# Two group norms of a hybrid encoder layer, by ones products over high and low parts of the squares

## The chip, the core and the metric

The kernel runs on one NeuronCore of one Trainium2 chip. The metric is the device time of one execution in microseconds (us); shown is the median of several runs. The engines are TensorE (PE: products, with its weight loads as PEld), VectorE (DVE), ScalarE (ACT), GpSimd (POOL), and SyncE (SP), which issues most of the DMAs.

## The reference

One layer of an encoder over 512 tokens of width 2048. A normed input is multiplied by one wide matrix, and its columns split into an attention group (8 heads of 128) and a recurrent group (LRU, width 1024), each with a gate. What matters here is the end of the layer, where each group's output is normed over its own 1024 features before the gate and the output projection:

```python
def rms_norm(x, w):
    xf = x.astype(jnp.float32)
    y = xf * lax.rsqrt(jnp.mean(xf * xf, axis=-1, keepdims=True) + EPS)
    return (y * w.astype(jnp.float32)).astype(x.dtype)
...
    mixed = jnp.concatenate([rms_norm(attn_out, attn_norm_w) * jax.nn.silu(g_attn),
                             rms_norm(lru_out, lru_norm_w) * jax.nn.silu(g_lru)], axis=-1)
    return x + jnp.einsum('bse,ed->bsd', mixed, w_out)
```

So for each group and each token, the squares of 1024 features are summed, and the features are scaled by one over the root of their mean plus EPS.

## The kernel before

Both groups are held with features on the 128 partitions and the 512 tokens along the free dimension: `hp` (four pairs of tiles, LRU) and `ap_` (four pairs, attention). A product of f32 precision is made of three products of rounded parts: a tile is split into a high part (a cast to fp32r, by ScalarE) and a low part (the rest, a subtraction by VectorE), and `mm3` (lines 153 to 155) multiplies high by high, high by low and low by high. Weights are loaded by SyncE (`wraw`, line 206) in chunks of two blocks and split the same way in `wsplit` (lines 218 and 219) into `wh` and `wl`, four buffers each in a pool; the splits are issued with raised priority.

TensorE's order is written out by hand: the generators of the big projections (`proj_feat`, `proj_tok`) yield after every six products, and `weave` runs a chain of smaller work between these steps; a chain that yields n lets n steps of the projection go by. The order of ScalarE, VectorE and GpSimd in the stages of this change is that of a planner, which goes by priority and expected times; `tc.high_priority()` raises the priority, and `tc.issue_after` (`behind` for several) puts an instruction behind another of its engine. In the last stage (`outputs`), all engines follow the written order.

The sums of squares come first. For the LRU group, `lru_squares` (lines 560 to 570) adds the squares of `hp` and leaves `sums["l"]`, 128x512; its last addition is on GpSimd (line 570). For the attention group, each head's `values` adds its squares to `sums["a"]` on GpSimd (line 753). What is left is the sum over the 128 partitions, for every token.

`group_rstd` (line 816) does this by four f32 products, one for every 128 tokens: 128 columns of the sums are the loaded weights, and a column of ones moves (line 820). The result has tokens on partitions, four columns. It is copied out of PSUM (line 824), and `rsqrt_mean` (lines 346 and 347) makes the root of the mean on GpSimd with a power of -0.5. Then `rows` (line 352) turns the four columns into a row that stands on all partitions: it splits them into a high and a low part (lines 357 and 358), spreads each over a diagonal of 128x512 (line 360, by the identity), multiplies both diagonals with ones (line 367) and copies the result into `gbc` (line 368). `normed` (line 831) multiplies a pair by `gbc`.

For the LRU group this runs in the chain `kv` (line 655) beside the projection of q: `group_rstd` stands behind the splits of the two key heads (`split_head`), four steps later `rows`. For the attention group it runs in `later` (line 1342) beside the projection of the last gate: two steps, `group_rstd`, four steps, `rows` and the scaling of two pairs, four steps, and the gate with its Silu (`gate`, line 807). `seven` (lines 844 to 852) splits and combines the normed groups for the output stage. The input's norm (`xstats`, line 371) uses `rsqrt_mean` and `rows` too.

GpSimd also issues DMAs that add blocks of `w_out` in DRAM (line 902), each behind the last of certain GpSimd instructions (`last_pool`, set in `rsqrt_mean` and at line 708).

Of the kernel before, what the change touches and what calls it, by code (L numbers as in the profile page):

```python
# [12 lines left out]
F32R = mybir.dt.float32r  # L13
AF = mybir.ActivationFunctionType
# [3 lines left out]
P = 128  # L18
SEQ = 512
DM = 2048  # L20
KT = DM // P
NT = SEQ // P
HD = 128
NH = 8
NKV = 2
G = NH // NKV
NB = 8
EPS = 1e-6
# [35 lines left out]
def hybrid_kernel(  # L64
# [20 lines left out]
    nc = tc.nc  # L85
# [4 lines left out]
    pools, order = {}, {"left": [], "right": []}  # L90

    def opened(name, side):
        pools[name] = tc.alloc_tile_pool(name=name, bufs=1, side=side, reuse_waits="tile")
        order[side].append(name)
        return pools[name]
# [22 lines left out]
    def nm(s):  # L118
        cnt[0] += 1
        return f"{s}_{cnt[0]}"  # L120
# [22 lines left out]
    def mm():  # L143
        return ps.tile([P, SEQ], F32, tag="mm", name=nm("mm"))

    def const(shape, name, dt=F32):
        return cp.tile(list(shape), dt, tag=name, name=name)

    def f(ap):
        return ap.bitcast(F32)  # L150
# [9 lines left out]
    ones = const([P, P], "ones")  # L160
    nc.gpsimd.memset(ones, 1.0)
    ones_r = const([P, P], "ones_r", F32R)
# [80 lines left out]
    def behind(those):  # L243
        stack = ExitStack()
        for ins in those:
            stack.enter_context(tc.issue_after(ins))
        return stack
# [52 lines left out]
    def in_order(v):  # L300
        return v.rearrange("p (t i r) -> p i t r", t=NT, i=NQ)
# [42 lines left out]
    def rsqrt_mean(dst, src, n, width):  # L344

        nc.gpsimd.tensor_scalar(dst, src, 1.0 / n, EPS, op0=ALU.mult, op1=ALU.add)
        last_pool[0] = nc.gpsimd.tensor_tensor(dst, dst, nhalf[:, :width], op=ALU.pow).ins
# [4 lines left out]
    def rows(dst, col, dg):  # L352

        shape = [P, NT, P]
        part = [const([P, NT], nm("part")) for _ in range(2)]
        parts = [dg() for _ in part]
        nc.vector.tensor_copy(part[0].bitcast(F32R), col)
        nc.vector.tensor_sub(part[1], col, part[0])
        for c, d in zip(part, parts):
            nc.vector.tensor_mul(  # L360
                d, ident[:, None, :].broadcast_to(shape), c[:, :, None].broadcast_to(shape)
            )
        yield
        pb = mm()
        for k, d in enumerate(parts):
            d = d.rearrange("p t q -> p (t q)")
            nc.tensor.matmul(pb, ones_r, d, start=k == 0, stop=k == 1)  # L367
        nc.vector.tensor_copy(dst, pb)
        yield
# [59 lines left out]
    def drain(fill):  # L429
        for _ in fill:  # L430
            pass
# [30 lines left out]
    sums = {}  # L462
# [97 lines left out]
    def lru_squares():  # L560

        hsum = pools["rot"].tile([P, 2, SEQ], F32, tag="hsum", name="hsum")
        nc.scalar.activation(hsum, hp[0], AF.Square)
        for pair in hp[1:]:
            yield 2
            sq = pools["rot"].tile([P, 2, SEQ], F32, tag="hsq", bufs=1, name=nm("hsq"))
            nc.scalar.activation(sq, pair, AF.Square)
            nc.vector.tensor_add(hsum, hsum, sq)
        sums["l"] = hsum[:, 0, :]
        nc.gpsimd.tensor_add(sums["l"], sums["l"], hsum[:, 1, :])  # L570
# [29 lines left out]
    def norm_rope(es, nh, tab):  # L600

        es = [e[:, : nh * HD].rearrange("p (h d) -> p h d", d=HD) for e in es]
        rs = []
        for e in es:
            r = pools["rot"].tile([P, nh], F32, tag=f"rr{nh}", bufs=NT, name=nm("rr"))
            for h in range(nh):
                sq = pools["rot"].tile([P, HD], F32, tag="sh", bufs=1, name=nm("sh"))
                nc.scalar.activation(sq, e[:, h, :], AF.Square, accum_out=r[:, h : h + 1])
            rsqrt_mean(r, r, HD, nh)
            rs.append(r)  # L610
        for t, (e, r) in enumerate(zip(es, rs)):
            sq = pools["rot"].tile([P, nh, HD], F32, tag="sq", bufs=2, name=nm("sq"))
            nc.vector.tensor_mul(e, e, r[:, :, None].broadcast_to([P, nh, HD]))
            for s in range(2):
                nc.vector.tensor_mul(
                    sq.rearrange("p h (a s d) -> p h a s d", s=2, d=32)[:, :, :, s, :],
                    e.rearrange("p h (a s d) -> p h a s d", s=2, d=32)[:, :, :, 1 - s, :],
                    tab[:, t, 1, :].rearrange("p (a s d) -> p a s d", s=2, d=32)[:, None, :, s, :]
                    .broadcast_to([P, nh, 2, 32]),
                )  # L620
            nc.vector.tensor_mul(e, e, tab[:, t, 0, :][:, None, :].broadcast_to([P, nh, HD]))
            nc.vector.tensor_add(e, e, sq)
        return es

    kth, ktl = [None] * NKV, [None] * NKV
# [5 lines left out]
    def sent(es, nh, *us):  # L631

        us = us or [
            pools["rot"].tile([P, NQ, 2, NT, B], F32, tag="uq", bufs=2, name=nm("uq"))
            for _ in range(nh // 2)
        ]
        for n, u in enumerate(us):
            for t, e in enumerate(es):
                blocks(u, t, e[:, 2 * n : 2 * n + 2].rearrange("p h d -> p (h d)"))
            yield  # L640
            asides.append(put_aside(u, "qd", 5))

    def landed(aside_):

        to = pools["qkv"].tile([P, NQ, 2, NT, B], F32, tag="lq", bufs=2, name=nm("lq"))
        bring_back(to, aside_)
        return to

    def split_head(pair, k, hi, lo):
        src = pair[:, :, k]  # L650
        hi, lo = (in_order(v) for v in (hi, lo))
        nc.scalar.copy(hi, src)
        nc.vector.tensor_sub(lo, src, f(hi))

    def kv(es):
        turned_k = sent(norm_rope(es, NKV, rk), NKV)
        yield 20
        opened("wx", "right")
        for t in range(NT):
            vv = es[t][:, NKV * HD :]  # L660
            vt = aside(
                lambda *a: pools["qkv"].tile(*a, tag="v", bufs=NT, name=nm("v")), 2 * NKV * HD // H
            )
            vh[t], vl[t] = vt[:, 0, :], vt[:, 1, :]
            nc.scalar.copy(vh[t], vv)
            nc.vector.tensor_sub(vl[t], vv, f(vh[t]))
        yield from lru_squares()
        yield 2
        drain(turned_k)
        yield 6  # L670
        pair = landed(asides.pop(0))
        for h in range(NKV):
            yield (12, 4)[h]
            kt = pools["qkv"].tile([P, 2, SEQ], F32R, tag="kt", bufs=NKV, name=nm("kt"))
            kth[h], ktl[h] = kt[:, 0, :], kt[:, 1, :]
            split_head(pair, h, kth[h], ktl[h])
        r = group_rstd(sums["l"], "r_l", NB * P)
        yield 4
        drain(rows(
            gbc, r,  # L680
            lambda: pools["rope"].tile([P, NT, P], F32R, tag="kv", bufs=NT, name=nm("kv")),
        ))

    qs = {}

# [127 lines left out]
    def fin_s(shape=(P, SEQ), dt=F32):  # L813
        return pools["fin"].tile(list(shape), dt, tag="s", bufs=2, name=nm("s"))

    def group_rstd(src, name, n):

        pr = mm()
        for t in range(NT):
            nc.tensor.matmul(  # L820
                pr[:, t : t + 1], src[:, t * P : (t + 1) * P], ones[:, 0:1], start=True, stop=True
            )
        r = const([P, NT], name)
        nc.vector.tensor_copy(r, pr[:, :NT])
        rsqrt_mean(r, r, n, NT)
        return r

    gbc = const([P, SEQ], "gbc")

    def normed(pair):  # L830
        nc.vector.tensor_mul(pair, pair, gbc[:, None, :].broadcast_to([P, 2, SEQ]))
# [22 lines left out]
    def aside(tile_of, n):  # L854

        t = tile_of([P, n * H + 16], F32R)
        return t[:, 8 : 8 + n * H].rearrange("p (n e) -> p n e", e=H)
# [475 lines left out]
    def build(i, pair, parts):  # L1333
        mixed[i][1] = parts
        seven(pair, *parts)
# [4 lines left out]


    def later():
        yield 2
        with tc.high_priority():
            r = group_rstd(sums["a"], "r_a", NH * HD)
        yield 4
        with tc.high_priority():
            drain(rows(gbc, r, lambda: fin_s((P, NT, P), F32R)))
        for pair in ap_[:2]:
            normed(pair)  # L1350
        yield 4
        todo = gate(late, ap_[:2], R_AN, fin_s)
        for _ in range(3):
            yield next(todo)
        build(4, ap_[0], [hring.tile([P, 7, H], F32R, name=nm(t)) for t in ("mh", "ml")])
        yield from todo
        for pair in ap_[2:]:
            normed(pair)
# [78 lines left out]
```

## Time and profile before

| what | value |
|---|---|
| time, median of 3 runs | 631.11 us (630.88 to 631.38) |
| the profiled execution: time | 631.51 us |
| its span, first to last instruction | 629.7 us |
| PE, DVE, ACT, POOL busy, share of the span | 99%, 78%, 55%, 17% |
| mean granted TensorE clock | 0.998 |

A line of the profile names the engine, the line of the kernel and the operation, then output and inputs by the program's names, shapes and how many; L820 is line 820. A timeline has the start in us from the beginning of the span, the duration, and in brackets the idle time before it with what ended it. A view of waits has who waited for whom, us in total, how many times, and the longest. Matmuls are pipelined, so their durations overlap: the distance from start to start is what one costs.

### The profile page before, as it was taken

What the parts mean: (1) busy time and instruction counts of PE and PEld (TensorE: products, weight loads), DVE (VectorE), ACT (ScalarE), POOL (GpSimd) and SP (SyncE); (2) the same over time, 40 slices, a digit from 0 to 9 for tenths busy, and PEclk for the clock granted to TensorE, in tenths of its full rate; (3) what the DMA queues carried; (4) which work ended last, traced back from release to release, by engine and by line L of the source; (5) the groups of instructions that cost most, each with busy time, mean ns of one, the idle gap of its engine ahead of it and who ended that gap; (6) DMA issues with size and microseconds to landing.
All of it is one profiled execution on the core that took longest, in us unless ns stands there. A gap on an engine that the chain in (4) does not pass through costs nothing.

```text
span 629.7 us, 8304 instructions
## 1 busy us (share of the span) xinstructions
PE 623.8 (99%) x2771; PEld 514.4 (82%) x2771; DVE 491.2 (78%) x796; ACT 348.5 (55%) x612; POOL 104.0 (17%) x137
## 2 busy tenths in 40 slices
PE   9999999999999999999999999999999999999997
PEld 6888888888888888888888888888888888888885
DVE  5967979986699874987887888549978866886875
ACT  3764899379936812555475447435445633443441
POOL 0000210112003631622122232100310001010010
PEclk9999999999999999999999999999999999999999
DMA  8877676859774599489668646924995777896262
GB/s 286 286 225 235 176 195 174 177 137 194 235 233 135 170 250 233 100 209 272 190 166 250 201 142 192 263 72 130 238 236 187 212 251 243 286 320 235 68 200 100
DMA packets 73594, 127.61 MB, mean 203 GB/s; under 512 B 6616, under 2 KB 29264, under 8 KB 73552
## 3 DMA queue, kind: packets, MB, share of 16 engines
q1 hardware_dynamic: 65664, 109.65, 55.7%
q0 software_dynamic: 7712, 17.31, 14.4%
q8 instruction: 21, 0.34, 0.2%
q10 hardware_dynamic: 176, 0.14, 0.1%
q14 instruction: 21, 0.17, 0.1%
HBM read 110.29 MB, written 37.75 MB: 235 GB/s over the span
## 4 chain that ended last, share of the span: by engine, by line
PE 97%; DMA 1%; DVE 0%; SPq 0%; ACT 0%; issue 0%; DVEq 0%
PE pj L154 21%; PE pj L153 20%; PE pj L155 20%; PE mm L1026 14%; PE pj L1026 10%; PE mm L155 4%; PE mm L153 3%; PE mm L154 3%; DMA wr<-in_w_in_dram 1%; PE mm L253 0%; PE mm L820 0%; PE mm L367 0%; SPq L240 0%; DVE wl L219 0%; DVE cb L1057 0%; SPq L206 0%
## 5 line engine op out<-in xcount | busy, mean ns | idle before, releaser
L153 PE MATMUL pj<-x,wh 128*128 128x512 f32 x376 | 146.9, 391 | 0.0
L154 PE MATMUL pj<-x,wh 128*128 128x512 f32 x376 | 146.6, 390 | 0.2 <-DVE x L261 0.2
L155 PE MATMUL pj<-x,wl 128*128 128x512 f32 x376 | 146.3, 389 | 0.0
L218 ACT CAST wh<-wr 128x512 fp32r<-128x512 f32 x143 | 85.6, 617 | 95.6 <-PE pj L154 36.7
L219 DVE TENSOR_TENSOR wl<-wr,wh 128x512 fp32r<-128x512 f32 x144 | 100.1, 722 | 20.0 <-ACT wh L218 18.7
L878 ACT CAST wh<-wr 128x1024 fp32r<-128x1024 f32 (+1 forms) x72 | 60.7, 860 | 75.0 <-PE mm L1026 35.4
L879 DVE TENSOR_TENSOR wl<-wr,wh 128x1024 fp32r<-128x1024 f32 (+1 forms) x72 | 68.7, 984 | 30.1 <-ACT wh L878 30.0
L154 PEld LDWEIGHTS pj<-x,wh 128*128 128x128 f32 x376 | 70.6, 188 | 15.2 <-DVE x L261 0.6
L155 PEld LDWEIGHTS pj<-x,wl 128*128 128x128 f32 x376 | 70.6, 188 | 14.8
L153 PEld LDWEIGHTS pj<-x,wh 128*128 128x128 f32 x376 | 70.6, 188 | 14.8
L153 PE MATMUL pj<-wh,x 128*128 128x512 f32 x192 | 74.8, 390 | 0.0
L155 PE MATMUL pj<-wh,x 128*128 128x512 f32 x192 | 74.7, 389 | 0.0
L154 PE MATMUL pj<-wl,x 128*128 128x512 f32 x192 | 74.7, 389 | 0.0
L902 POOL DMA_DIRECT2D t<-in_w_out_dram x40 | 33.7, 904 | 143.4 <-DMA t<-in_w_out_dram 99.9
L1026 PE MATMUL mm<-wh,ml 128*128 128x512 f32 x128 | 49.8, 389 | 0.0
L1026 PE MATMUL mm<-wh,mh 128*128 128x512 f32 x128 | 49.8, 389 | 0.0
L1026 PE MATMUL mm<-wl,mh 128*128 128x512 f32 x128 | 49.8, 389 | 0.0
L154 PEld LDWEIGHTS pj<-wl,x 128*128 128x128 f32 x192 | 36.0, 188 | 7.5
L153 PEld LDWEIGHTS pj<-wh,x 128*128 128x128 f32 x192 | 36.0, 188 | 7.5
L155 PEld LDWEIGHTS pj<-wh,x 128*128 128x128 f32 x192 | 36.0, 188 | 7.4
L708 POOL TENSOR_SCALAR p<-p,sm 128x512 f32<-128x512 f32 x32 | 24.2, 759 | 90.0 <-DVE sm L707 90.0
L1026 PE MATMUL pj<-wh,mh 128*128 128x512 f32 x96 | 37.4, 389 | 0.0
(209 smaller groups left out, 1035.6 us busy)
## 6 DMA issues: line engine op xcount, KB each, us to landing
wr<-in_w_in_dram SPq DMA_DIRECT2D x71, 512.0 KB, 5.0
wr<-in_w_out_dram SPq DMA_DIRECT2D x24, 512.0 KB, 5.3
t<-in_w_out_dram POOLq DMA_DIRECT2D x40, 256.0 KB, 7.3
wr<-t SPq DMA_DIRECT2D x40, 256.0 KB, 5.5
pd<-u SPq DMA_DIRECT2D x16, 512.0 KB, 3.0
pt<-pd SPq DMA_DIRECT2D x64, 128.0 KB, 3.9
t<-in_w_out_dram SPq DMA_DIRECT2D x24, 256.0 KB, 5.4
t<-t SPq DMA_DIRECT2D x16, 256.0 KB, 5.4
```

The source lines that it names most:

```text
L153: nc.tensor.matmul(acc, lh, rh, start=start, stop=False)
L154: nc.tensor.matmul(acc, lh, rl, start=False, stop=False)
L155: nc.tensor.matmul(acc, ll, rh, start=False, stop=stop)
L218: copy(hi, raw[:, k, :]).ins,
L219: nc.vector.tensor_sub(lo, raw[:, k, :], f(hi)).ins,
L708: last_pool[0] = nc.gpsimd.tensor_scalar(p, p, sm, 0.0, op0=ALU.mult, op1=ALU.add).ins
L878: nc.scalar.copy(hi[:, to], b)
L879: nc.vector.tensor_sub(lo[:, to], b, f(hi[:, to]))
L902: nc.gpsimd.dma_start(dst, src, accum_op=ALU.add)
L1026: nc.tensor.matmul(dst[s], lh[:, ts_], rh, start=i == 0 and j == 0, stop=i == 7 and j == 2)
```

## The change

`group_rstd` goes. Its place is taken by two functions. `halved` splits the 128x512 sums into a high part (a copy into fp32r on ScalarE) and a low part (a subtraction on VectorE). `spread` multiplies both with a 128x128 block of ones into one bank of PSUM, so that every partition receives the sum of all; ScalarE takes the root of the mean plus EPS out of PSUM into `gbc`, with EPS from a constant tile, and VectorE takes the reciprocal in place, in four pieces of 128 tokens. `rows` stays for the input's norm.

In the LRU group the parts are made where `group_rstd` stood, pinned behind the split of the second key head, and `spread` stands where `rows` stood, four steps later. In the attention group the parts are made at the start of `later`, `spread` stands where `group_rstd` stood, and where `rows` stood there is nothing left. The parts use the buffers that the diagonals of `rows` used. The constant `eps` is 48 floats wide.

```diff
     def split_head(pair, k, hi, lo):
         src = pair[:, :, k]
         hi, lo = (in_order(v) for v in (hi, lo))
-        nc.scalar.copy(hi, src)
-        nc.vector.tensor_sub(lo, src, f(hi))
+        return nc.scalar.copy(hi, src).ins, nc.vector.tensor_sub(lo, src, f(hi)).ins
...
-            split_head(pair, h, kth[h], ktl[h])
-        r = group_rstd(sums["l"], "r_l", NB * P)
+            those = split_head(pair, h, kth[h], ktl[h])
+        parts = halved(
+            sums["l"],
+            lambda: pools["rope"].tile([P, SEQ], F32R, tag="kv", bufs=NT, name=nm("kv")),
+            those,
+        )
         yield 4
-        drain(rows(
-            gbc, r,
-            lambda: pools["rope"].tile([P, NT, P], F32R, tag="kv", bufs=NT, name=nm("kv")),
-        ))
+        spread(gbc, parts, NB * P)
...
-    def group_rstd(src, name, n):
-
-        pr = mm()
+    eps = const([P, 48], "eps")
+    nc.gpsimd.memset(eps, EPS)
+
+    def halved(src, tile_of, those=()):
+
+        hi, lo = tile_of(), tile_of()
+        with behind(those):
+            nc.scalar.copy(hi, src)
+            nc.vector.tensor_sub(lo, src, f(hi))
+        return hi, lo
+
+    def spread(dst, parts, n):
+
+        pb = mm()
+        for k, part in enumerate(parts):
+            nc.tensor.matmul(pb, ones_r, part, start=k == 0, stop=k == 1)
+        nc.scalar.activation(dst, pb, AF.Sqrt, scale=1.0 / n, bias=eps[:, :1])
         for t in range(NT):
-            nc.tensor.matmul(
-                pr[:, t : t + 1], src[:, t * P : (t + 1) * P], ones[:, 0:1], start=True, stop=True
-            )
-        r = const([P, NT], name)
-        nc.vector.tensor_copy(r, pr[:, :NT])
-        rsqrt_mean(r, r, n, NT)
-        return r
+            ts_ = slice(t * P, (t + 1) * P)
+            nc.vector.reciprocal(dst[:, ts_], dst[:, ts_])
...
     def later():
+        with tc.high_priority():
+            parts = halved(sums["a"], lambda: fin_s(dt=F32R))
         yield 2
         with tc.high_priority():
-            r = group_rstd(sums["a"], "r_a", NH * HD)
+            spread(gbc, parts, NH * HD)
         yield 4
-        with tc.high_priority():
-            drain(rows(gbc, r, lambda: fin_s((P, NT, P), F32R)))
         for pair in ap_[:2]:
             normed(pair)
```

## The prediction

> **What bounds the kernel now.** I read the page first: the span, the busy line and the head of the chain that ended last.
>
> ```profile
> span 629.7 us, 8304 instructions
> ...
> PE 623.8 (99%) x2771; PEld 514.4 (82%) x2771; DVE 491.2 (78%) x796; ACT 348.5 (55%) x612; POOL 104.0 (17%) x137
> ...
> PE 97%; DMA 1%; DVE 0%; SPq 0%; ACT 0%; issue 0%; DVEq 0%
> ```
>
> TensorE is busy for 623.8 of 629.7 us, and 97% of the chain that sets the end is TensorE. Busy alone would not prove that it never waits, so next I read the view of waits, for PE and for its weight loads (PEld):
>
> ```profile
> PE mm L1144 <- POOL ones L161: 1.1, 1, 1.1
> ...
> PEld mm L155 <- DVE q L653: 0.3, 1, 0.3
> ```
>
> The first row is the warm-up at the very start. After the pipeline has filled, TensorE waits nowhere for more than 0.3 us. So here the time is what TensorE has to issue: an instruction taken out of its stream is worth its whole slot, and anything else counts only if it makes TensorE wait. Both groups' norms stand in such a stream. The timeline of PE around the LRU group's norm, then around the attention group's (start, duration, instruction):
>
> ```profile
> 231.72 0.40 PE L155 MATMUL pj<-wh,x 128*128 128x512 f32 x1
> 231.96 0.95 PE L820 MATMUL mm<-ones,hsum 128*128 128x1 f32 x8
> ...
> 233.08 0.39 PE L154 MATMUL pj<-wl,x 128*128 128x512 f32 x1
> ...
> 238.33 0.62 PE L367 MATMUL mm<-kv,ones_r 128*128 128x512 f32 x2
> 238.79 0.40 PE L153 MATMUL pj<-wh,x 128*128 128x512 f32 x1
> ```
>
> ```profile
> 430.10 0.40 PE L155 MATMUL pj<-x,wl 128*128 128x512 f32 x1
> 430.33 0.95 PE L820 MATMUL mm<-ones,asum 128*128 128x1 f32 x8
> ...
> 431.45 0.39 PE L154 MATMUL pj<-x,wh 128*128 128x512 f32 x1
> ...
> 436.71 0.62 PE L367 MATMUL mm<-s,ones_r 128*128 128x512 f32 x2
> ```
>
> Durations of neighbours overlap, so the price of an instruction is read from starts, and that of an ordinary 128x512 product from twelve in one row of the chain (start, us):
>
> ```profile
> 472.71 2.72 PE mm L1026 x12
> ```
>
> That is 0.227 us each. What the reader is to see: the four products of line 820 stand in the stream as eight TensorE instructions, and although each moves a single column (128x1) they hold it for most of a microsecond.
>
> **The change part by part.** *TensorE, LRU group.* From the last product before line 820 (231.72) to the second after it (233.08) are 1.36 us; two ordinary starts take 2 x 0.227 = 0.45. Line 820 costs 0.91 us, and it goes. The two products of ones with the halves take the place and the form of line 367: from 238.33 to 238.79 are 0.46 us for the two, an ordinary slot each, as now. Saved: 0.91.
>
> *TensorE, attention group.* 430.10 to 431.45 are 1.35 us, less 0.45: 0.90. The two products move up from 436.71 to this place, at an unchanged price. Saved: 0.90. Together 0.91 + 0.90 = **1.81 us**. This is the only term that lies on the path by itself.
>
> *Are the halves there when TensorE asks?* The sums end early:
>
> ```profile
> L570 POOL TENSOR_TENSOR hsum<-hsum x1: 1622/1622/1622, 206.1 to 206.1; 128x512 f32<-128x512 f32 x1
> ...
> 422.73 1.30 POOL L753 TENSOR_TENSOR asum<-asum,p 128x512 f32<-128x512 f32 x1 [15.41 <-ACT p L752]
> ```
>
> Splitting costs one ScalarE copy and one VectorE subtraction; the same pair on 128x512 runs in every head's split:
>
> ```profile
> L652 ACT CAST q<-lq 128x512 fp32r<-128x512 f32 x8 | 4.9, 621 | 6.2 <-PE mm L155 6.2
> ...
> L653 DVE TENSOR_TENSOR q<-lq,q 128x512 fp32r<-128x512 f32 x8 | 5.3, 676 | 0.0
> ...
> 226.86 1.25 DVE L653 TENSOR_TENSOR kt<-lq,kt 128x512 fp32r<-128x512 f32 x2
> ```
>
> LRU: the sum has been there since 207.7; the halves are pinned behind the last key split, which VectorE ends at 228.1, so they are due near 230, and TensorE asks at 237.4. Seven us of cover. Attention: the sum ends at 424.03; plus 0.62, 0.68 and 0.2 for two hand-overs is 425.5, against 429.4, when TensorE asks (430.33 less the 0.91). Four us of cover, if both engines take the pair at once. Cost: nothing. Behind the copy on ScalarE and the subtraction on VectorE stand the weights' splits, for which the products wait; their slack follows.
>
> *ScalarE.* One Sqrt per group out of PSUM, 128x512, and whatever table it needs.
>
> ```profile
> L706 ACT ACTIVATE p<-mm,mx 128x512 f32<-128x512 f32 x32 | 21.9, 686 | 23.1 <-DVE mx L704 23.0
> ...
> L546 ACT ACT_TABLE_LOAD  x4: 1283/1283/1283, 85.8 to 169.0; - x4
> ...
> 269.47 1.28 ACT L706 ACT_TABLE_LOAD   x1
> ...
> 433.31 1.32 ACT L218 CAST wh<-wr 128x512 fp32r<-128x512 f32 x2 [0.37 <-ACT mh L851]
> 434.65 1.28 ACT L807 ACT_TABLE_LOAD   x1
> ```
>
> The Sqrt tables of line 546 are loaded at 169.0 and no other load precedes 269.47, so the LRU Sqrt costs 0.69 alone. In the attention group it stands between Exp and Silu: one load more, 1.28 + 0.69 = 2.0 us. In that stage ScalarE is half idle (view of windows: start:end, length, busy time of PE, PEld, DVE, ACT, POOL):
>
> ```profile
> 425.00:473.00 48.00, 48.00 (x217) 39.82 (x216) 42.08 (x64) 24.15 (x33) 8.01 (x10) 1.00 0.77 204
> ```
>
> What is queued behind the Sqrt there is the copy of the next weights, at 433.31; a Sqrt begun at 430 is over by 432.0. Cost: nothing.
> [...]
>
> *VectorE.* It loses, per group, three instructions on 128x4 (lines 824, 357, 358), two of line 360 and the copy of line 368:
>
> ```profile
> 433.01 0.17 DVE L357 CAST part<-r_a 128x4 fp32r<-128x4 f32 x1 [1.21 <-POOL r_a L347]
> ...
> 434.03 1.29 DVE L360 TENSOR_TENSOR s<-ident,part 128x512 fp32r<-128x512 f32 x2
> ...
> 438.71 0.69 DVE L368 COPY gbc<-mm 128x512 f32<-128x512 f32 x1
> ```
>
> These are 3 x 0.17 + 1.29 + 0.69 = 2.49 us. It gains one subtraction (0.68) and four reciprocals on 128x128. No row has that shape:
>
> ```profile
> L707 DVE RECIPROCAL sm<-sm x32: 118/155/167, 271.6 to 394.2; 128x1 f32<-128x1 f32 x32
> ...
> L446 DVE RECIPROCAL lc<-lc 128x16 f32<-128x16 f32 x1 | 0.3, 253 | 0.0
> ```
>
> From 1 to 16 elements a reciprocal grows by 253 - 155 = 98 ns, 6.5 ns an element; 128 elements give 155 + 127 x 6.5 = 0.98 us, four 3.9. The lower end is one ordinary pass over 128x512, 0.69 as line 368; the upper takes the shortest single one, (253 - 118) / 15 = 9.0 ns, 1.26 each, 5.0 in all. I take 3.9, since both rows are reciprocals. Net per group 0.68 + 3.9 - 2.49 = +2.1 us, between -1.1 and +3.2.
> [...]
>
> What this pushes. LRU stage, VectorE:
>
> ```profile
> 239.72 3.50 DVE L831 TENSOR_TENSOR hs<-hs,gbc 128x1024 f32<-128x1024 f32 x3
> ...
> 247.15 0.69 DVE L219 TENSOR_TENSOR wl<-wr,wh 128x512 fp32r<-128x512 f32 x1 [2.19 <-ACT wh L218]
> 252.89 0.69 DVE L613 TENSOR_TENSOR ev<-ev,rr 128x512 f32<-128x512 f32 x1 [5.05 <-POOL rr L347]
> ...
> 256.73 0.69 DVE L613 TENSOR_TENSOR ev<-ev,rr 128x512 f32<-128x512 f32 x1 [0.30 <-POOL rr L347]
> ...
> 267.09 1.29 DVE L653 TENSOR_TENSOR q<-lq,q 128x512 fp32r<-128x512 f32 x2
> ```
>
> VectorE idles 2.19 + 5.05 = 7.2 us before 252.89; the reciprocals less the copy are 3.9 - 0.69 = 3.2 of it. Covered. Attention stage:
>
> ```profile
> 431.39 0.41 DVE L849 TENSOR_TENSOR t<-hs,t 128x256 f32<-128x256 f32 x1
> ...
> 435.24 1.29 DVE L219 TENSOR_TENSOR wl<-wr,wh 128x512 fp32r<-128x512 f32 x2
> ...
> 441.72 1.29 DVE L219 TENSOR_TENSOR wl<-wr,wh 128x512 fp32r<-128x512 f32 x2
> ```
>
> Here VectorE is nearly full (42.08 of 48). A chunk of weights is four steps of six products, 24 x 0.227 = 5.44 us. Line 820 stands two steps into one, so the next begin near 433.9, 439.8 (line 367 lies between) and 445.2. The low halves for the latter two end at 436.5 and 443.0: slack 3.3 and 2.2 us. The added 2.1 is offset by the 1.21 that VectorE spends waiting for GpSimd's power, which disappears; so some 0.9 us net, below the slack. Cost: nothing, but this is the thinnest cover.
>
> *GpSimd and the rest.* GpSimd loses two pairs of lines 346 and 347 and gains one memset beside that of line 165, behind the ones that TensorE awaits at the start; its DMA issues were pinned behind the power and may go out a little sooner. Nobody waits for them in these stages. Six constant columns of four floats go and a constant of 48 floats comes; I take it that no pool moves. Zero both ways.
>
> *Sum.* The profiled execution took 631.51 us, its span 629.7 with 1.8 around it, 0.40 above the median of 631.11. 631.51 - 1.81 = 629.70; from the median **629.30**.
>
> **The rivals.**
> *Weights late (same, or a small gain).* If all four reciprocals run ahead of a weight split in the attention stage, at the upper price the added 3.2 us less a slack of 2.2 (1.3, as TensorE comes 0.9 sooner) is a wait of up to 1.9 us; at my price about 0.8. Against it: four pieces, between which a split fits. Time 631.11 - 1.81 + 0.8 = 630.1, up to 631.2.
> *The products wait for the halves (the change does not do what it says: the slot becomes a wait).* VectorE's run before its wait at 433.01 ends at 431.8 (line 849). If the low half is put at the end of that run, which follows TensorE and so comes 0.9 sooner, it is there at 430.9 + 0.7 = 431.6; TensorE asks at 429.4 and, being in order, stands for 2.2 us: 631.11 - 1.81 + 2.2 = 631.5. It decides from a half later than 429.4. For it: one in-order queue. Against: four us and a raised priority.
> *First scores late (slower).* The place is 267.09: VectorE runs without a break from 256.73 to there, and the first score already waits 0.3 us for line 653. The order of VectorE is planned, and the four scalings by gbc (line 831, 1.22 us each) follow the reciprocals. If they no longer fit before 252.89 and are put into that run, each holds TensorE 1.22 us. It decides from the second: 2 x 1.22 is more than 1.81. All four: 4.9 - 1.8 = +3.1, 634.2. For it: the reciprocals end 3.2 us later than the copy did. Against: 7.2 idle us take that.
>
> **How the numbers follow.** Forecast 0.66, with 628.8 to 629.8 (the runs shown lie 0.5 apart). Weights late 0.14, halves late 0.08, scores late 0.12. A measurement here can tell about 0.2%, 1.26 us, from no change; the border is 629.85. Faster: the forecast and a little of the second, 0.68. Same: 0.21. Slower: 0.11. The range is 628.8 to 631.2: the forecast and the two that give part of it back, 0.88 less their upper tails (some 0.07); the slower rival is left out.
>
> **What would show it.** Right: no rows with 128x1 products in 225:245 and 425:473; two products with ones_r near 237.4 and 429.4, between ordinary starts; PE's waits without a new row; one table load more, before the attention Sqrt; eight reciprocals of 128x128 near 0.98 us, and the first score 0.9 us sooner, everything behind 440 1.8 us sooner. Wrong: PE waiting for lines 219, 653 or the new subtraction, or PE's gap at 267 to 268 grown. The forecast fails as a whole if line 820's slots do not close up, that is, if the same idle time turns up elsewhere in TensorE's stream.

## The result and the profile after

| | median (lowest to highest) | profiled execution | its span |
|---|---|---|---|
| before, measured beside it | 631.20 us (630.82 to 632.94) | 631.51 us | 629.7 us |
| after | 630.21 us (629.86 to 630.94) | 630.30 us | 628.2 us |

The ratio is 0.9980, 95% interval 0.9975 to 0.9986: faster by 0.9 to 1.6 us, where 1.8 were forecast. The page of the changed kernel answers to the page of before:

```profile
span 628.2 us, 8273 instructions
...
PE 622.0 (99%) x2755; PEld 512.5 (82%) x2755; DVE 494.6 (79%) x794; ACT 353.1 (56%) x618; POOL 101.4 (16%) x134
...
PE 98%; DVE 1%; issue 0%; DVEq 0%; POOL 0%; POOLq 0%
```

TensorE has 16 instructions fewer: four products of line 820, eight instructions, in each of two groups. It is still the bound, but VectorE now holds 1% of the chain that sets the end, where it held 0%. A new wait is behind that. The view of waits of the changed kernel (us in total, how many, the longest):

```profile
PEld pj L155 <- DVE wl L219: 1.3, 2, 0.8
...
PE pj L155 <- DVE wl L219: 0.3, 1, 0.3
PEld mm L155 <- DVE q L652: 0.3, 1, 0.3
```

TensorE and its weight loads wait for line 219, the low half of a weight chunk. (Of the 1.3 us in the first row, 0.8 belong to the stage of the attention group's norm; the other 0.5 lie in the start-up, between 30 and 60 us.) That is what "Weights late" would look like. To see what it costs, I cut the span at three places that both kernels have: the ones products of the input's norm (line 367), the first ones products of the attention group, and the first product of the output stage. First the chain of before (start, us; its third row, 472.71, stands in the prediction), then that of after:

```profile
50.58 0.46 PE mm L367 x2
...
430.49 0.79 PE mm L820 x8
```

```profile
50.30 0.46 PE mm L367 x2
...
429.28 0.46 PE mm L831 x2
...
471.21 2.72 PE mm L1035 x12
```

| stretch, us | before | after | saved |
|---|---|---|---|
| start to the input's norm | 50.58 | 50.30 | 0.28 |
| input's norm to attention's ones products (holds the LRU norm) | 379.91 | 378.98 | 0.93 |
| attention's ones products to the first output product | 42.22 | 41.93 | 0.29 |
| first output product to the end | 157.0 | 157.0 | 0 |

The change adds one memset to the start-up, and the ten traces of this case put its end anywhere between 49.56 and 50.94 us, so its 0.28 us is taken for scatter. The LRU group gave its whole slot, 0.93 us. The attention group gave 0.29, so some 0.6 us are lost there. PE's timeline in that stretch shows one place:

```profile
437.98 0.39 PE L154 MATMUL pj<-x,wh 128*128 128x512 f32 x1
438.70 0.50 PE L155 MATMUL pj<-x,wl 128*128 128x512 f32 x1 [0.33 <-DVE wl L219]
439.04 0.40 PE L153 MATMUL pj<-x,wh 128*128 128x512 f32 x1
```

From 437.98 to 439.04 two starts take 1.06 us; ordinary ones take 2 x 0.227 = 0.45. The wait costs 0.61 us, and that is the loss. (The bracket shows 0.33 because it counts from the modelled end of the product before.) VectorE's timeline says what it did instead of the split:

```profile
432.58 0.69 DVE L856 TENSOR_TENSOR t<-hs 128x512 f32<-128x512 f32 x1
...
433.85 0.95 DVE L861 TENSOR_TENSOR ml<-hs,mh 128x768 fp32r<-128x768 f32 x1
434.71 3.39 DVE L835 RECIPROCAL gbc<-gbc 128x128 f32<-128x128 f32 x4
438.01 2.43 DVE L219 TENSOR_TENSOR wl<-wr,wh 128x512 fp32r<-128x512 f32 x4
```

The four reciprocals stand in one unbroken row of 3.39 us, and four weight splits stand behind it. ScalarE's timeline shows when the root that the reciprocals read was there, and when the high halves that the splits need were done:

```profile
428.42 1.28 ACT L807 ACT_TABLE_LOAD   x1
429.71 0.64 ACT L807 ACTIVATE s<-ev 128x512 f32<-128x512 f32 x1
430.36 1.28 ACT L832 ACT_TABLE_LOAD   x1
431.66 0.69 ACT L832 ACTIVATE gbc<-mm,eps 128x512 f32<-128x512 f32 x1
432.24 1.13 ACT L218 CAST wh<-wr 128x512 fp32r<-128x512 f32 x2
...
434.69 1.28 ACT L807 ACT_TABLE_LOAD   x1
```

One gate's Silu (line 807) was put ahead of the Sqrt (line 832). The table goes to Silu, to Sqrt and back to Silu: three loads where before had one. The Sqrt is over at 432.35, but the planner's order has VectorE do parts of `seven` (lines 856 to 861) until 434.71 before the reciprocals. The high halves (line 218) were done by 433.37, so a split at 434.71 would have been over by about 435.4, at the 0.69 us that line 219 takes for one, well ahead of TensorE's 438.2.

Two theories follow. **The row**: the raised priority puts all four reciprocals in front of the splits, and splits between them would remove the wait. **The loads**: the two extra table loads make the stage late, and without them the wait would go, while the order of VectorE is innocent. In the expectations below, the first is called "Late weights" and the second "Tables"; "Loose stream" is a third, by which the removed slots are worth less than their starts say, without any one wait.

### The profile page after: what moved, and what is told of

The parts are those of the page before. It is cut to its first block, busy times and chain, and to the rows that moved or that the text cites. A ratio compares the mean times of both kernels' runs of the same rounds, so it can differ in the third digit from the quotient of the medians.

```text
span 628.2 us, 8273 instructions
## 1 busy us (share of the span) xinstructions
PE 622.0 (99%) x2755; PEld 512.5 (82%) x2755; DVE 494.6 (79%) x794; ACT 353.1 (56%) x618; POOL 101.4 (16%) x134
## 4 chain that ended last, share of the span: by engine, by line
PE 98%; DVE 1%; issue 0%; DVEq 0%; POOL 0%; POOLq 0%
PE pj L155 20%; PE pj L153 20%; PE pj L154 20%; PE mm L1035 14%; PE pj L1035 10%; PE mm L155 4%; PE mm L153 3%; PE mm L154 3%; PE pj L388 1%; PE mm L253 1%; PE mm L1153 1%; DVE gbc L835 1%; DVE wl L219 0%; DVE cb L1066 0%; PE mm L831 0%
```

## The experiments

All are edits of the changed kernel. Times of before beside them were 631.47 us (630.62 to 632.52) for the first four, and 631.55 us (630.76 to 632.65) for the others. Single medians move by some tenths, so what is weighed is mostly the two stretches of the table above, which in equal code repeat to some hundredths, but for one case named below.

### Only the LRU group changed

`group_rstd` and `rows` stay for the attention group (in this run and the next, the constant `eps` is 24 floats wide instead of 48):

```diff
-        with tc.high_priority():
-            parts = halved(sums["a"], lambda: fin_s(dt=F32R))
         yield 2
         with tc.high_priority():
-            spread(gbc, parts, NH * HD)
+            r = group_rstd(sums["a"], "r_a", NH * HD)
         yield 4
+        with tc.high_priority():
+            drain(rows(gbc, r, lambda: fin_s((P, NT, P), F32R)))
```

> Only the LRU group is changed; the attention group keeps the four products with one column and the diagonals. Late weights (the time is two slots of TensorE saved, less one wait for a weight's low half at 438 us, behind the four reciprocals): the LRU slot goes and no wait comes, so 0.91 to 0.95 us less than before, about 630.3 against 631.2, and no wait of TensorE for line 219 around 438. Loose stream (the removed slots are worth less than their starts say, in both groups alike, without any one wait): half of the measured 1.0 us, so 0.5 less, 630.7.

Measured: 630.21 us (629.70 to 630.55), ratio 0.9979 (0.9970 to 0.9987). The chain:

```profile
50.29 0.46 PE mm L367 x2
...
429.28 0.79 PE mm L841 x8
...
471.50 2.72 PE mm L1047 x12
```

The first stretch is 378.99 us, as in the full change; the second, left alone, is 42.22, as in before. TensorE waits nowhere in it. The LRU half is worth 0.92 us without any loss.

### Only the attention group changed

The reverse edit, with `group_rstd` and `rows` in the LRU chain.

> Only the attention group is changed; the LRU group keeps the old way. Late weights: 0.90 us saved, 0.61 lost in the wait for the weight's low half at about 439, so 0.3 less than before, 630.9, with the wait in the trace. Loose stream: 0.5 less, 630.7, and no wait that belongs to the group.

Measured: 630.92 us (630.43 to 631.34), ratio 0.9990 (0.9981 to 0.9999). The waits between 400 and 480 us:

```profile
PEld pj L155 <- DVE wl L219: 0.7, 1, 0.7
...
PE pj L155 <- DVE wl L219: 0.3, 1, 0.3
```

The stretches are 379.92 and 41.91: the wait is there without the LRU half, and the saving of this half is 0.31 us instead of the 0.90 of the forecast. So the two halves do not disturb each other, and the loss belongs to the attention group alone.

### The reciprocals at plain priority

Products and Sqrt keep their raised priority, the attention group's reciprocals lose it:

```diff
         with tc.high_priority():
-            spread(gbc, parts, NH * HD)
+            spread(gbc, parts, NH * HD, False)   # without the reciprocals
+        turn_over(gbc)                           # the four reciprocals
         yield 4
```

> The changed kernel with the attention group's four reciprocals at plain priority instead of raised priority; nothing else. Late weights: the low halves of the next weights go ahead of them, the wait at 438 is gone, and the full 1.8 us are saved: 629.4 against 631.2, or 0.6 less than the changed kernel. Tables (what delays is the extra table loads of ScalarE, with a Silu put ahead of the Sqrt; the reciprocals don't matter): the loads stay, so the wait stays, 630.2. Loose stream: 630.2 too, without a wait.

Measured: 629.56 us (629.37 to 630.35), ratio 0.9972 (0.9961 to 0.9982). VectorE's timeline, then ScalarE's, then the chain:

```profile
434.58 1.29 DVE L219 TENSOR_TENSOR wl<-wr,wh 128x512 fp32r<-128x512 f32 x2
...
441.40 0.95 DVE L840 RECIPROCAL gbc<-gbc 128x128 f32<-128x128 f32 x1
...
442.55 1.76 DVE L840 RECIPROCAL gbc<-gbc 128x128 f32<-128x128 f32 x2
...
446.62 0.95 DVE L840 RECIPROCAL gbc<-gbc 128x128 f32<-128x128 f32 x1
```

```profile
428.28 1.28 ACT L807 ACT_TABLE_LOAD   x1
...
430.23 1.28 ACT L832 ACT_TABLE_LOAD   x1
...
434.58 1.28 ACT L807 ACT_TABLE_LOAD   x1
```

```profile
429.15 0.46 PE mm L831 x2
...
470.43 2.72 PE mm L1040 x12
```

A split now takes the place where the row of reciprocals began, the reciprocals begin 6.7 us later and stand in three parts, and TensorE waits for nobody in the stage. The second stretch is 41.28 us, 0.94 below before: the whole slot. (The first stretch is 379.17 us here, 0.2 more than in the changed kernel. Weight loads wait there 0.3 us, once, for line 526, which in before runs from 64 to 160 us, far ahead of the edited stage; whether that is scatter was not tried.) All three table loads are still there, within 0.14 us of their times. So loads alone do not make the wait; the row is needed for it.

### Twice the row

Two of the four reciprocals are executed three times in place, at raised priority, so that the row has eight pieces (a reciprocal taken three times gives the value of one, but for rounding):

```diff
-            spread(gbc, parts, NH * HD)
+            spread(gbc, parts, NH * HD, False)
+            turn_over(gbc, 3)                    # three times for t < 2
```

> The changed kernel with two of the four reciprocals of the attention group done three times in place (the result is the same), so eight pieces stand in the row of four, 3.4 us more on VectorE ahead of the same weight splits. Late weights: TensorE's wait grows by the same 3.4 us, from 0.6 to about 4.0, and the time is 633.6, 2.4 above before. Tables and loose stream: VectorE is off the path, 630.2 as now.

Measured: 635.51 us (634.14 to 636.64), ratio 1.0060 (1.0046 to 1.0075), more than expected. VectorE, PE, and the view of windows (start:end, length, busy time of PE, PEld, DVE, ACT, POOL, granted clock, DMA share, GB/s):

```profile
433.94 6.63 DVE L841 RECIPROCAL gbc<-gbc 128x128 f32<-128x128 f32 x8
```

```profile
437.21 0.39 PE L154 MATMUL pj<-x,wh 128*128 128x512 f32 x1
441.17 0.67 PE L155 MATMUL pj<-x,wl 128*128 128x512 f32 x1 [3.57 <-DVE wl L219]
441.63 0.63 PE L153 MATMUL pj<-x,wh 128*128 128x512 f32 x1
...
444.62 0.46 PE L154 MATMUL pj<-x,wh 128*128 128x512 f32 x1
```

```profile
439.00:442.00 3.00, 0.83 (x2) 0.70 (x3) 3.00 (x5) 0.00 (x0) 0.00 (x0) 0.89 0.00 0
442.00:446.00 4.00, 4.00 (x13) 3.15 (x12) 4.00 (x7) 1.05 (x1) 0.00 (x0) 0.66 0.74 248
```

The row grew by 6.63 - 3.39 = 3.24 us, and the wait in the brackets from 0.33 to 3.57, by 3.24. Every added piece went into the wait, at full price. On top of it, the eight products from 441.17 to 444.62 start 0.43 us apart instead of 0.227, which is 3.45 - 8 x 0.227 = 1.63 us more, while the granted clock of the window from 442 to 446 is 0.66. That second part no theory had. Both together, 4.87, are what the second stretch grew by (46.75 against 41.93: 4.82). The execution with the trace is the fastest of the six. In three of the others, of 635.95 to 636.64 us, the mean granted clock of the whole execution was 0.993 where this one had 0.997; they left no trace, so whether their trains of slow products were longer is not shown.

### The changed kernel again

The same code beside the next three, on one chip.

> The changed kernel as it is, beside the next three on one chip. Late weights: 1.2 us less than before by its trace (0.94 for the LRU group, 0.3 for the attention group), with TensorE's wait for line 219 near 438. If the wait came by chance in the first trace, it is not there and the time is 629.5.

Measured: 630.05 us (629.64 to 631.29), ratio 0.9977 (0.9968 to 0.9986). The stretches are 378.93 and 41.92, and the wait is there again with 0.3 us for PE and 0.8 for its weight loads. The loss belongs to the program's order and is no accident of one execution.

### The last gates' Silu behind the Sqrt

Priorities stay as in the change; the Silus are pinned behind the attention group's Sqrt:

```diff
+            root.append(spread(gbc, parts, NH * HD))  # spread returns its Sqrt
...
+                    for ins in root:                  # in gate, at the Silu
+                        stack.enter_context(tc.issue_after(ins))
```

> The changed kernel with the last gates' Silus pinned behind the attention group's Sqrt on ScalarE: one table load less, and the Sqrt some 2 us sooner; the reciprocals keep their raised priority and stay together ahead of the next weight splits. Late weights: they end about 2 us sooner, so the low halves are there in time, the wait is gone, 629.4, and the stretch from the group's products to the first output product falls from 41.93 to about 41.3 us. Reciprocals alone (their standing ahead of the splits is enough, whenever they start): the wait stays, 41.9, 630.2.

Measured: 629.56 us (629.38 to 630.23), ratio 0.9969 (0.9958 to 0.9980). ScalarE's timeline, then VectorE's:

```profile
429.00 1.28 ACT L836 ACT_TABLE_LOAD   x1
430.36 0.69 ACT L836 ACTIVATE gbc<-mm,eps 128x512 f32<-128x512 f32 x1
...
432.88 1.28 ACT L811 ACT_TABLE_LOAD   x1
```

```profile
433.16 3.38 DVE L844 RECIPROCAL gbc<-gbc 128x128 f32<-128x128 f32 x4
436.46 1.22 DVE L219 TENSOR_TENSOR wl<-wr,wh 128x512 fp32r<-128x512 f32 x2
```

And the chain:

```profile
429.86 0.46 PE mm L835 x2
...
471.14 2.72 PE mm L1044 x12
```

One load is gone. The four reciprocals are the same unbroken row ahead of the splits, but it begins 1.55 us sooner (433.16 for 434.71) and the split at 436.46 instead of 438.01, although the products themselves came 0.58 us later in this execution. The products start at 429.86 and the output stage at 471.14: 41.28 us, the whole slot again, with no wait in the stage. So my theory was too strong: standing ahead of the splits is not enough either. The wait needs both, a row of 3.3 us ahead of the splits and its late start; taking away either one removes it.

### One reciprocal instead of four

```diff
-        for t in range(NT):
-            ts_ = slice(t * P, (t + 1) * P)
-            nc.vector.reciprocal(dst[:, ts_], dst[:, ts_])
+        nc.vector.reciprocal(dst, dst)
```

> The changed kernel with one reciprocal on 128x512 in place of four on 128x128, in both groups. Pieces help (a split fits between them, as the prediction said): with one instruction the wait grows, to 1.5 us or more, 631. Pieces idle (the planner issues the four in one row anyway): one instruction of about 3.3 us in place of 3.39, the wait is the same 0.6 or a little shorter, 630.2.

Measured: 629.79 us (629.33 to 630.24), ratio 0.9973 (0.9962 to 0.9984); the ranges of this and of the changed kernel overlap. VectorE:

```profile
434.40 3.34 DVE L833 RECIPROCAL gbc<-gbc 128x512 f32<-128x512 f32 x1
437.66 2.42 DVE L219 TENSOR_TENSOR wl<-wr,wh 128x512 fp32r<-128x512 f32 x4
```

One instruction that nothing can split behaves as the four did: the same length, the same splits behind it, the same wait, and 41.91 us for the stretch. The four pieces made no opening for a split.

### Plain priority and Silu behind the Sqrt together

Both edits at once.

> The changed kernel with both edits: Silus behind the Sqrt, and the attention group's reciprocals at plain priority. Late weights: no wait, as with the priority alone, so the stretch from the group's products to the first output product is 41.3 us and the time 629.4; the second edit buys nothing more. If the priority only moved the wait elsewhere, it shows here as a wait for another line.

Measured: 629.58 us (629.40 to 629.92), ratio 0.9970 (0.9959 to 0.9982); stretches 378.97 and 41.28, no wait. It adds nothing to either edit alone: there is one wait to remove, and either removes it. The three mended versions have medians of 629.56 to 629.58 us, about 0.3% below before. Against the changed kernel they gain 0.65 us by the stretches and some 0.5 by the medians, whose ranges overlap.

## Why the prediction was right, and where it was not

**What bounds, and the slots: right.** The forecast took 0.91 and 0.90 us for line 820. Measured where nothing hinders, they are 0.92 to 0.93 (LRU) and 0.94 (attention). The new pair costs what line 367 cost, 0.46 us. With the wait removed, the three mended versions are 1.9 to 2.0 us below before by the medians, where 1.81 were forecast: the sum holds for an order without that wait.

**Halves in time: right.** VectorE's timeline of the changed kernel, with the first reciprocals and the next place that was feared:

```profile
227.33 0.69 DVE L824 TENSOR_TENSOR kv<-hsum,kv 128x512 fp32r<-128x512 f32 x1
...
238.48 3.39 DVE L835 RECIPROCAL gbc<-gbc 128x128 f32<-128x128 f32 x4 [3.23 <-ACT gbc L832]
...
251.66 0.69 DVE L613 TENSOR_TENSOR ev<-ev,rr 128x512 f32<-128x512 f32 x1 [3.91 <-POOL rr L347]
...
423.88 0.68 DVE L824 TENSOR_TENSOR s<-asum,s 128x512 fp32r<-128x512 f32 x1
```

The low halves are there at 228.0 and 424.6, and TensorE asks at 237.1 and 429.1. "Products wait for the halves" did not occur, with 9 and 4.5 us to spare. The 0.2 us for two hand-overs was the author's estimate; in the attention group the first took 0.04 us here (the sum ends on GpSimd at 422.80, its copy on ScalarE starts at 422.84), and the low half began 0.42 us after that copy ended at 423.46, behind other work of VectorE.

**First scores late: did not occur.** VectorE still idles 3.91 us before 251.66, so the LRU group's reciprocals fitted into the idle time as reckoned. The first score's wait is 0.3 us, as before (for line 652; the same subtraction was line 653 in before).

**The reciprocal: right within a tenth for one piece.** 0.98 us was forecast, from 1 and 16 elements, and 3.9 for four; four in a row took 3.39, and the row of the line gives:

```profile
L835 DVE RECIPROCAL gbc<-gbc x8: 894/900/953, 238.5 to 437.2; 128x128 f32<-128x128 f32 x8
```

VectorE's busy time of the whole page went from 491.2 to 494.6, +1.7 a group against +2.1.

**The failed step** is the attention stage on VectorE: "some 0.9 us net, below the slack. Cost: nothing, but this is the thinnest cover", with "four pieces, between which a split fits" against the rival. Two things were wrong in it. First, net work in a stage was set against the slack of the splits, but what counts is what stands ahead of one split at one moment: at 434.71 the split had some 2.8 us left (over by 435.4, asked for at 438.2) and the planner put 3.3 us of raised reciprocals ahead of it. In before, most of the removed work and the wait for GpSimd stood ahead of that split too, but were over when it began at 435.24, and the copy of line 368, counted as removed, stood behind it (438.71). In the changed kernel that time went to parts of `seven` (the row at 433.85 ends them), the last 2.4 us of it after the Sqrt was over at 432.35, and the reciprocals came on top. Why the planner put those parts first was not tried. Second, that pieces can be interleaved says nothing of whether they are: they have the same raised priority and become ready together. The run with one reciprocal shows that the cut was worth nothing; the run with plain priority shows what an order with the splits first is worth, 0.65 us (41.93 - 41.28).

**A smaller miss helped it.** "One load more" on ScalarE, and a Sqrt over by 432.0, assumed that the Silu stays behind the Sqrt. Silu went first, so there were two loads more and the Sqrt was over at 432.35. The run with the Silu behind it had its Sqrt over at 431.05 and no wait. Why the planner chose Silu first was not tried.

So the outcome is the rival "Weights late", at 0.6 us where 0.8 were named, and its 630.1 us is nearer to 630.21 than the forecast of 629.3. That the size came so near is luck: the rival worked its 0.8 out for the chunk asked for near 445.2, with a slack of 1.3 us. The wait came at the chunk before it, where the same sum, 2.1 us against a slack of 3.3 - 0.9 = 2.4, gives no wait; the later chunk's low halves were over by 440.44, and nobody waited for them. The result also lies outside the 628.8 to 629.8 us that the forecast named for its own case; it lies in the whole range because that took the rivals in. The mechanism that brings the gain was right, and so was the place where it could be given back; the choice between the two was wrong.

## What to carry to other kernels

In this kernel, with TensorE busy for 99% of the span, instructions taken out of its stream were worth their start-to-start distance where no wait took the place: eight starts with one column each cost 0.90 to 0.91 us, as much as four full products of 0.227, and without them the stretch was 0.92 to 0.94 us shorter. But when work is moved to another engine, do not balance work added against work removed over a stage: find the next item that TensorE waits for, and count only what will stand ahead of it, with the latest time at which that work can start. A raised priority on something that nobody awaits soon can take exactly that place.

## What the runs showed of the hardware

In one run of this case a wait of TensorE cost more than itself. In the run with the double row, after 3.57 us without work, eight products started 0.43 us apart, at a granted clock of 0.66 in the window from 442 to 446 us (0.89 from 439 to 442), before the distance was 0.227 again. The wait of 0.33 us in the changed kernel had no such train: the first start after it is followed by the next after 0.34 us, from there on the distance is 0.22 to 0.24, and the granted clock was 1.00 from 436 to 446 us. No run shows how long a wait has to be for such a train.

In this case the time of a reciprocal on VectorE grew with its elements, and cutting it was almost free: 3.34 us for 128x512, 3.39 for four of 128x128 in a row. From one piece of 953 ns to the full width it grew by (3340 - 953) / 384 = 6.2 ns an element, where the prediction had 6.5 from rows of 1 and 16 elements.

A table load showed no pause beside it, neither ahead of it nor behind it: in the changed kernel, the load at 430.36 starts 0.01 us after the Silu before it ends and ends at 431.64, and the Sqrt starts at 431.66.
